# Thirty-two 128x128 turns a layer leave TensorE: VectorE turns 32x32 blocks and a trip through DRAM puts them in place

## The chip, the cores and the metric

The kernel runs on one core of a Trainium2 chip. That core has five engines, each with its own instruction queue: TensorE (PE in the profile; its weight loads are PEld), VectorE (DVE), ScalarE (ACT), GpSimd (POOL) and SyncE (SP), which here only issues DMAs. Sixteen DMA engines move data between DRAM and the on-chip memory; a DMA is issued by SP, ACT or POOL and waits in that engine's queue until its semaphores are met. Matmul results land in PSUM, from which ACT or DVE must copy them.

The metric is the device time of one execution, in microseconds, as a median over several executions. Before the change it is 1737.33 us, from 1736.18 to 1737.69 us.

## The reference

The kernel computes two layers of a decoder trunk over a sequence of 512 positions and 1024 channels. In each layer a normalized input goes through one wide projection, whose columns feed three branches and three sets of gates; the gated sum of the branches is projected and added, and a gated MLP with a short convolution follows. Two of the branches matter here.

```
# recurrence (8 heads of 64):  S_t = S_{t-1} (diag(w_t) - kk_t^T (a_t kk_t)) + v_t^T k_t ;  y_t = S_t r_t
y = rwkv7_scan(r, decay, k, v, kk, a)
mean, var = over the 64 channels of a head
y = (y - mean) * rsqrt(var + 64e-5) * lnx_g + lnx_b
y = y + sum(r * k * r_k) * v
return y * g

# retention (4 heads, q and k of 64 channels, chunks of 128 positions)
q, k = rotary(q), rotary(k) / 8
scores = (q_i . k_j) * decay_in[i, j]     # within a chunk
inner  = scores @ v
kv     = k^T (v * k_dec)                  # carried from chunk to chunk
cross  = q @ R_prev * q_dec
y = (inner + cross) normalized, times silu(g)
```

In both there is a turn from positions on the partitions to channels on the partitions. The recurrence's `y` is normalized with positions on the partitions, since a head's channels then lie along a row; the branch projection wants channels on the partitions. The rotation of q and k works with positions on the partitions, since the tables of cosines are per position; the products `q . k` contract over channels and want those on the partitions.

## The kernel before

Activations are kept as features: 128 channels on the partitions, 512 positions along a row. Weights come from DRAM in pieces of 128x512 (256 KB) through three raw buffers (`wr`), are cut by ACT (`wh` or `sh`, line 134) and DVE (`wl` or `sl`, line 135) into a high and a low part in a reduced-precision format, and each product of a weight piece and an activation is three matmuls (line 151, `mm3`). Almost the whole time goes into these. Weight pieces are prepared ahead of their use by a fixed number of pieces, two during the recurrence, three or more later.

The order on each engine is set when the program is built: the scheduler of the framework places instructions by a simulated time, except where the code pins them (`keep_in_program_order`, in the code often `po`). The engines then run their queues strictly in that order, waiting on semaphores.

In each layer the work around the change runs so:

- **Recurrence** (`rwkv`). Eight steps, c = 0 to 7, of 64 positions. A step's chain goes PE, DVE (`XB`), PE, ACT (`U`), PE, DVE (the state `S`, lines 628 and 629), and the next step's first products read `S` (line 563). Between the parts of a chain stand fillers, each one weight piece of 12 matmuls of the gates' and retention's projections (`fill`, lines 151). After every odd step the 128 finished positions `y` are normalized: DVE takes sums (lines 639 to 646), POOL raises to the power -1/2 (`rs`, line 648), DVE multiplies (line 649). The four tiles `y` stay in memory.
- **Rotation** (`rotate`, lines 780 to 785). While the recurrence runs, four tiles of 128 positions of q and k are rotated on DVE into `ro`, using a second tile `rb_`.
- **Read-out** (`rwkv_out`). After the recurrence, PE runs four groups of 24 products for the spatial gating branch (`sgu_v`), and between them, for each of four blocks of 128 channels, four transposes of `y` into one PSUM tile (line 661), a copy out by ACT with scale and bias (line 663), and DVE's additions and products (lines 664 and 667).
- **Retention's heads** (`ret_heads`). Some ten microseconds later PE turns the four `ro` tiles in sixteen transposes (line 796) into `qF` and `kF`, which ACT and DVE copy out (line 798). The rows of the retention (`ret_row`, line 817) read them.

So a layer has 32 transposes of 128x128 on PE. In layer 2 everything is repeated with the same order.

The last layer's MLP already has a turn by DVE's 32x32 blocks and a trip through DRAM (`turn_x`, lines 963 to 968): DVE transposes blocks of 32x32 (`xz`), SP writes them to DRAM in pieces of 512 bytes (`xr<-xz`, line 966) and reads them back in pieces of 128 bytes (`xt<-xr`, line 968).

Of the kernel before, what the change touches and what calls it, by code (L numbers as in the profile page):

```python
# [8 lines left out]
F32 = mybir.dt.float32  # L9
F32R = mybir.dt.float32r  # L10
AF = mybir.ActivationFunctionType
# [7 lines left out]
NC = 4  # L19
# [28 lines left out]
class Emit:  # L48
# [343 lines left out]
        return self.fp.tile(list(shape), dt, name=self.nm(n), tag="a")  # L392


    def rwkv(self, l, nst):
        nc, V, A, a = self.nc, self.nc.vector, self.nc.scalar, self.a
        T, P = nc.tensor, nc.gpsimd
# [3 lines left out]
        po = self.tc.keep_in_program_order if l == 0 else lambda i: i  # L401
# [33 lines left out]
        for i in range(2):  # L435
            x = self.u(n="wax")
            for h in range(2):
                o, s = x[64 * h:64 * h + 64, :], wa[64 * i:64 * i + 64, :]
# [12 lines left out]
        hv, po = [slice(0, 64), slice(64, 128)], self.tc.keep_in_program_order  # L451
# [105 lines left out]

        Vt, yT, mh = [None] * 8, [], [(m, h) for m in range(4) for h in range(2)]  # L560

        def mm(o, l, r, start=False):
            po(T.matmul(o, l, r, start=start, stop=True, skip_group_check=True))  # L563
# [17 lines left out]
        for c in range(8):  # L581
            if c % 2 == 0:
                y = self.r(n="y")
# [22 lines left out]
            for i in (0, 4, 5, 6, 7, 1, 2, 3):  # L606
                for h in range(2):
                    m, o = i % 4, 1 - h
# [14 lines left out]
            if c < 7:  # L623
                f = F[:, :, c:c + 1].to_broadcast([128, 4, 64])
# [17 lines left out]
            sq = self.r(n="ysq")  # L642
# [4 lines left out]
            rs = self.small((128, 8), "rs8")  # L647
            nc.gpsimd.tensor_tensor(rs, s2, self.c("mhalf")[:, 0:8], op=POW)
            V.tensor_tensor(h8(y), h8(y), rs.unsqueeze(2).to_broadcast([128, 8, 64]), op=MUL)
            yT.append(y)  # L650
        return yT, bv, gd

    def rwkv_out(self, l, yT, bv, gd):
        nc, V, A, T, a = self.nc, self.nc.vector, self.nc.scalar, self.nc.tensor, self.a
        gw, gx = self.split(self.gup, self.f), self.split(gd, self.f)
        self.yrw = []
        for m in range(4):
            ms = slice(m * 128, m * 128 + 128)
            pt = self.sm()
            for c in range(NC):  # L660
                self.tc.keep_in_program_order(T.transpose(pt[:, c * 128:c * 128 + 128], yT[c][:, ms], self.c("ident")))  # L661
            t = self.f(n="yF")
            A.activation(t, pt, AF.Identity, scale=self.p("lg", m), bias=self.p("lb", m))
            V.tensor_tensor(t, t, bv[m], op=ADD)
            pg = self.sm()
            self.mm3(pg, (gw[0][:, ms], gw[1][:, ms]), gx, True, True)
            V.tensor_tensor(t, t, pg, op=MUL)
            self.yrw.append(self.split(t, self.f))
            yield
# [96 lines left out]
    def rotate(self, l, qs):  # L766

        nc, V, a, po = self.nc, self.nc.vector, self.a, self.tc.keep_in_program_order
        for c in range(NC):
            s = qs.pop(0)  # L770
            if c % 2 == 0:
                tab = [self.u((128, 2, 256), n="tab") for _ in range(2)]
                for i in range(2):
                    nc.scalar.dma_start(tab[i], a["rot"][:, i, c:c + 2, :])
            src = s.rearrange("p (h e d) -> p h e d", e=2, d=32)
            Cc, Ss = [t[:, c % 2, :].rearrange("p (h d) -> p h d", d=32) for t in tab]
            o = self.u(n="ro")
            ov = o.rearrange("p (h e d) -> p h e d", e=2, d=32)
            b = self.u((128, 8, 2, 32), n="rb_")
            po(V.tensor_tensor(ov, src, Cc.unsqueeze(2).to_broadcast([128, 8, 2, 32]), op=MUL))  # L780
            po(V.tensor_tensor(b[:, :, 0, :], src[:, :, 1, :], Ss, op=MUL))
            yield
            po(V.tensor_tensor(b[:, :, 1, :], src[:, :, 0, :], Ss, op=MUL))
            po(V.tensor_tensor(ov[:, :, 0, :], ov[:, :, 0, :], b[:, :, 0, :], op=SUB))
            po(V.tensor_tensor(ov[:, :, 1, :], ov[:, :, 1, :], b[:, :, 1, :], op=ADD))
            self.ro.append(o)
            yield

    def ret_heads(self):

        A, V, T, po = self.nc.scalar, self.nc.vector, self.nc.tensor, self.tc.keep_in_program_order
        self.qF, self.kF = [], []
        for j in range(4):
            pt = self.sm((128, 4, 128))
            for c in range(NC):
                po(T.transpose(pt[:, c, :], self.ro[c][:, j * 128:j * 128 + 128], self.c("ident")))
            t = self.r((128, 4, 128), n="qF" if j < 2 else "kF")
            (V.tensor_copy if j % 2 else A.copy)(t, pt)
            (self.qF if j < 2 else self.kF).append(t)
        self.kd = []  # L800
        for c in range(NC - 1):
            kd = self.r((128, 4, 64), n="kd")
            V.tensor_tensor(kd, self.ro[c][:, 256:512].rearrange("p (h d) -> p h d", d=64),
                            self.c("kdec").unsqueeze(2).to_broadcast([128, 4, 64]), op=MUL)
            self.kd.append(kd)
# [396 lines left out]
```

## Time and profile before

| | us |
|---|---|
| median of three executions | 1737.33 |
| the profiled execution, its own time | 1736.33 |
| its span, first to last instruction | 1734.6 |
| PE busy | 1725.1 |
| DVE busy | 1121.2 |
| ACT busy | 775.8 |
| POOL busy | 151.9 |
| recurrence with its normalizations, layer 1 | about 214 to 317 |
| read-out and heads, layer 1 | about 344 to 381 |
| the same in layer 2 | about 1074 to 1177 and 1204 to 1241 |

A row of a timeline gives the start in us from the beginning of the span, the duration, the engine, the line, the operation, the tile written and the tiles read, and in brackets the idle time of the engine before it and what ended that. A row of a line or a tile gives the least, the median and the greatest duration in ns. Matmuls are pipelined: the distance between two starts, not the duration, is what one costs PE.

### The profile page before, as it was taken

What the parts mean: (1) busy time and instruction counts of PE and PEld (TensorE: products, weight loads), DVE (VectorE), ACT (ScalarE), POOL (GpSimd) and SP (SyncE); (2) the same over time, 40 slices, a digit from 0 to 9 for tenths busy, and PEclk for the clock granted to TensorE, in tenths of its full rate; (3) what the DMA queues carried; (4) which work ended last, traced back from release to release, by engine and by line L of the source; (5) the groups of instructions that cost most, each with busy time, mean ns of one, the idle gap of its engine ahead of it and who ended that gap; (6) DMA issues with size and microseconds to landing.
All of it is one profiled execution on the core that took longest, in us unless ns stands there. A gap on an engine that the chain in (4) does not pass through costs nothing.

```text
span 1734.6 us, 27538 instructions
## 1 busy us (share of the span) xinstructions
PE 1725.1 (99%) x10544; PEld 1421.0 (82%) x10544; DVE 1121.2 (65%) x1933; ACT 775.8 (45%) x1329; POOL 151.9 (9%) x168
## 2 busy tenths in 40 slices
PE   9999999999999999999999999999999999999998
PEld 7888877888888888888888888778888888888887
DVE  6777645568658777753357785455686698876432
ACT  6554444534345444443255635445343454443322
POOL 1011000002300000000021210000132000000010
PEclk9999999999999999999999999999999999999999
DMA  5234433424543223233332344234154444432431
GB/s 178 86 98 140 134 98 94 134 66 163 162 145 98 97 97 96 69 116 112 116 116 73 98 146 124 92 115 129 59 176 143 152 128 122 121 110 73 152 99 54
DMA packets 124900, 198.64 MB, mean 115 GB/s; under 512 B 29408, under 2 KB 35296, under 8 KB 124768
## 3 DMA queue, kind: packets, MB, share of 16 engines
q1 hardware_dynamic: 110064, 164.15, 30.1%
q10 hardware_dynamic: 10224, 18.05, 3.1%
q0 software_dynamic: 4480, 14.68, 2.6%
q8 instruction: 83, 1.36, 0.3%
q14 instruction: 49, 0.40, 0.1%
HBM read 177.95 MB, written 18.87 MB: 113 GB/s over the span
## 4 chain that ended last, share of the span: by engine, by line
PE 97%; DMA 1%; DVE 1%; ACT 0%; issue 0%; ACTq 0%; DVEq 0%
PE acc L151 86%; PE sm L151 4%; PE sm L563 2%; PE sm L817 1%; PE sm L507 1%; DMA wr<-wall 0%; PE sm L922 0%; PE sm L590 0%; DMA x<-xT 0%; PE sm L479 0%; PE sm L468 0%; PE sm L467 0%; PE sm L845 0%; PE sm L661 0%; PE sm L872 0%
## 5 line engine op out<-in xcount | busy, mean ns | idle before, releaser
L151 PE MATMUL acc<-lo,sh 128*128 128x512 f32 x1108 | 432.6, 391 | 0.0
L151 PE MATMUL acc<-hi,sh 128*128 128x512 f32 x1108 | 431.6, 390 | 0.0
L151 PE MATMUL acc<-hi,sl 128*128 128x512 f32 x1108 | 430.5, 389 | 0.0
L134 ACT CAST sh<-wr 128x512 fp32r<-128x512 f32 (+1 forms) x385 | 235.4, 616 | 390.4 <-PE acc L151 286.8
L135 DVE TENSOR_TENSOR sl<-wr,sh 128x512 fp32r<-128x512 f32 (+1 forms) x385 | 263.4, 688 | 177.9 <-ACT sh L134 108.0
L151 PEld LDWEIGHTS acc<-lo,sh 128*128 128x128 f32 x1108 | 208.0, 188 | 43.9 <-issue 0.7
L151 PEld LDWEIGHTS acc<-hi,sl 128*128 128x128 f32 x1108 | 208.0, 188 | 43.3
L151 PEld LDWEIGHTS acc<-hi,sh 128*128 128x128 f32 x1108 | 208.1, 188 | 42.7 <-issue 0.2
L151 PE MATMUL acc<-lo,wh 128*128 128x512 f32 x588 | 232.9, 396 | 0.8 <-DVE lo L210 0.6
L151 PE MATMUL acc<-hi,wl 128*128 128x512 f32 x588 | 229.7, 391 | 0.0
L151 PE MATMUL acc<-hi,wh 128*128 128x512 f32 x588 | 229.6, 390 | 0.0
L135 DVE TENSOR_TENSOR wl<-wr,wh 128x512 fp32r<-128x512 f32 x195 | 141.8, 728 | 133.8 <-ACT wh L134 132.9
L134 ACT CAST wh<-wr 128x512 fp32r<-128x512 f32 x195 | 120.7, 619 | 218.4 <-PE acc L151 208.0
L151 PEld LDWEIGHTS acc<-lo,wh 128*128 128x128 f32 x588 | 110.5, 188 | 25.8 <-DVE lo L210 1.2
L151 PEld LDWEIGHTS acc<-hi,wl 128*128 128x128 f32 x588 | 110.4, 188 | 23.9 <-issue 0.7
L151 PEld LDWEIGHTS acc<-hi,wh 128*128 128x128 f32 x588 | 110.6, 188 | 22.2 <-issue 0.3
L151 PE MATMUL acc<-ah,sh 128*128 128x512 f32 x352 | 108.4, 389 | 0.0
L989 DVE TENSOR_TENSOR fu<-acc,rsF 128x512 f32<-128x512 f32 x88 | 60.8, 690 | 66.1 <-PE acc L151 66.0
L991 ACT ACTIVATE cv<-fu,pc 128x512 f32<-128x512 f32 x88 | 71.7, 816 | 47.6 <-DVE fu L989 45.1
L992 DVE SCALAR_TENSOR_TENSOR cv<-fu,pc,cv 128x511 f32<-128x511 f32 x88 | 65.7, 748 | 19.9 <-ACT cv L991 19.8
L151 PE MATMUL acc<-wl,hi 128*128 128x512 f32 x192 | 78.3, 408 | 0.0
L151 PEld LDWEIGHTS acc<-ah,sh 128*128 128x128 f32 x352 | 66.1, 188 | 13.6
(297 smaller groups left out, 2338.5 us busy)
## 6 DMA issues: line engine op xcount, KB each, us to landing
wr<-wall SPq DMA_DIRECT2D x488, 256.0 KB, 2.6
gd<-gth ACTq DMA_DIRECT2D x48, 256.0 KB, 2.9
gth<-gd POOLq DMA_DIRECT2D x48, 256.0 KB, 3.5
wr<-wdt SPq DMA_DIRECT2D x44, 256.0 KB, 2.8
wr<-wdn SPq DMA_DIRECT2D x40, 256.0 KB, 2.7
tab<-rot ACTq DMA_DIRECT2D x8, 256.0 KB, 3.5
xi<-xT SPq DMA_DIRECT2D x8, 256.0 KB, 3.3
xd<-xi POOLq DMA_DIRECT2D x8, 256.0 KB, 2.7
```

What stands on the lines that cost most here:

```text
L134: self.kept(self.nc.scalar.copy(hi[:, :n], raw[:, :n]))
L135: self.kept(self.nc.vector.tensor_tensor(lo[:, :n], raw[:, :n], hi[:, :n], op=SUB))
L151: i = self.nc.tensor.matmul(*x, **y, **kw)
L507: i = T.matmul(pK[hv[1 - h], j, :], bk[hv[h], c, 1, :], x[hv[h], c, :], start=True, stop=True)
L563: po(T.matmul(o, l, r, start=start, stop=True, skip_group_check=True))
L817: po(T.matmul(X[h][:, i, :], lhsT, rhs, start=new[h], stop=stop, skip_group_check=True))
L989: V.tensor_tensor(u, ps, self.rsF, op=MUL)
L991: A.activation(t, u, AF.Identity, scale=self.p("cw2", j), bias=self.p("cb", j))
L992: V.scalar_tensor_tensor(t[:, 1:], u[:, :511], self.p("cw1", j), t[:, 1:], op0=MUL, op1=ADD)
```

## The change

The four finished tiles `y` of the recurrence and the four rotated tiles `ro` are no longer kept for PE. As soon as one is finished, `to_dram` lets DVE transpose its sixteen 32x32 blocks per 32 positions in one instruction over 128x512, into a tile that is no longer needed (`ysq` or `rb_`), and POOL issues four DMAs, each of 32 partitions with 16 x 32 runs of 32 numbers (512 pieces of 128 bytes, 64 KB), that write the blocks to their places in a 512x512 array in DRAM (`tn`). Later, SP reads four tiles of 128 channels x 512 positions back from it for `yF`, and four for `qF` and `kF`, each a DMA of 256 KB. The transposes on PE and the copies out of PSUM by lines 663 (which becomes an in-place scaling of `yF`) and 798 go. Nothing else is computed differently.

```
+    def to_dram(self, z, src, d, c, eng):
+        self.nc.vector.transpose(z.rearrange("p (b t) -> p b t", t=32), src.rearrange("p (b f) -> p b f", f=32))
+        for q in range(4):
+            eng.dma_start(d.rearrange("(b f) t -> f b t", f=32)[:, :, 128 * c + 32 * q:128 * c + 32 * q + 32],
+                          z[32 * q:32 * q + 32].rearrange("f (b t) -> f b t", t=32))
+    def turned(self):
+        return self.dp.tile([512, 512], F32, name=self.nm("tn"))
...
-        Vt, yT, mh = [None] * 8, [], [(m, h) for m in range(4) for h in range(2)]
+        Vt, yT, mh = [None] * 8, self.turned(), [(m, h) for m in range(4) for h in range(2)]
...
             V.tensor_tensor(h8(y), h8(y), rs.unsqueeze(2).to_broadcast([128, 8, 64]), op=MUL)
-            yT.append(y)
+            self.to_dram(sq, y, yT, c // 2, nc.gpsimd)
...
-        self.yrw = []
-        for m in range(4):
+        self.yrw, ys = [], [self.f(n="yF") for _ in range(4)]
+        for m, t in enumerate(ys):
+            nc.sync.dma_start(t, yT[128 * m:128 * m + 128, :])
+        for m, t in enumerate(ys):
             ms = slice(m * 128, m * 128 + 128)
-            pt = self.sm()
-            for c in range(NC):
-                self.tc.keep_in_program_order(T.transpose(pt[:, c * 128:c * 128 + 128], yT[c][:, ms], self.c("ident")))
-            t = self.f(n="yF")
-            A.activation(t, pt, AF.Identity, scale=self.p("lg", m), bias=self.p("lb", m))
+            A.activation(t, t, AF.Identity, scale=self.p("lg", m), bias=self.p("lb", m))
...
+        self.qk = self.turned()
...
+            self.to_dram(b.rearrange("p h e d -> p (h e d)"), o, self.qk, c, nc.gpsimd)
             self.ro.append(o)
...
-            pt = self.sm((128, 4, 128))
-            for c in range(NC):
-                po(T.transpose(pt[:, c, :], self.ro[c][:, j * 128:j * 128 + 128], self.c("ident")))
             t = self.r((128, 4, 128), n="qF" if j < 2 else "kF")
-            (V.tensor_copy if j % 2 else A.copy)(t, pt)
+            self.nc.sync.dma_start(t.rearrange("p c t -> p (c t)"), self.qk[128 * j:128 * j + 128, :])
```

The lines of the changed file are 10 later in the recurrence, 8 or 9 later in the read-out and the rotation, 7 later from the heads on: line 648 is 658, line 649 is 659, 628 is 638.

The scheduler places the new instructions among the old ones. At three places of layer 1 (layer 2 has the same order) the queues read as follows; the first number of a row is the line, a tile's numbers are its buffers.

POOL during the recurrence, before: the four powers `rs`, one for each pair of steps, and then the first of the spatial gating branch's.

```order
L648 TENSOR_TENSOR rs_491_2543<-s_490_2540,con 128x8
L648 TENSOR_TENSOR rs_533_2851<-s_532_2848,con 128x8
L648 TENSOR_TENSOR rs_569_3151<-s_568_3148,con 128x8
L648 TENSOR_TENSOR rs_611_3431<-s_610_3428,con 128x8
L890 TENSOR_TENSOR brs_3835<-bve_3833,con 128x1
```

POOL at the same place with the change (`x4` is four DMAs).

```order
L399 DMA tn_2211<-ysq_2852 32x16x32 x4
L399 DMA tn_3193<-rb__583_3199 32x16x32 x2
L658 TENSOR_TENSOR rs_570_3162<-s_569_3159,con 128x8
L399 DMA tn_3193<-rb__583_3199 32x16x32 x2
L399 DMA tn_2211<-ysq_3157 32x16x32 x4
L399 DMA tn_3193<-rb__595_3308 32x16x32 x4
L399 DMA tn_3193<-rb__606_3398 32x16x32 x4
L658 TENSOR_TENSOR rs_613_3463<-s_612_3460,con 128x8
L399 DMA tn_3193<-rb__618_3491 32x16x32 x4
L399 DMA tn_2211<-ysq_3458 32x16x32 x4
```

Two DMAs of the first rotated tile now stand ahead of the third `rs`, and fourteen more between the third and the fourth.

DVE from the third normalization's sum to the state's update of step c = 6, before.

```order
L645 TENSOR_REDUCE s_568_3148<-ysq_3146 128x8
L646 TENSOR_SCALAR s_568_3148<-s_568_3148 128x8
L135 TENSOR_TENSOR wl_3270<-wr_3159,wh_3269 128x512
L780 TENSOR_TENSOR ro_3285<-qs_3115,tab_3177 128x512
L781 TENSOR_TENSOR rb__593_3286<-qs_3115,tab_3178 128x8x32
L649 TENSOR_TENSOR y_2854<-y_2854,rs_569_3151 128x512
L135 TENSOR_TENSOR wl_3312<-wr_3212,wh_3311 128x512
L783 TENSOR_TENSOR rb__593_3286<-qs_3115,tab_3178 128x8x32
L784 TENSOR_TENSOR ro_3285<-ro_3285,rb__593_3286 128x8x32
L628 TENSOR_TENSOR S_396<-S_396,sm_3233 128x256
```

The same stretch with the change.

```order
L655 TENSOR_REDUCE s_569_3159<-ysq_3157 128x8
L397 STREAM_TRANSPOSE rb__583_3199<-ro_3198 128x512
L656 TENSOR_SCALAR s_569_3159<-s_569_3159 128x8
L135 TENSOR_TENSOR wl_3292<-wr_3175,wh_3291 128x512
L789 TENSOR_TENSOR ro_3307<-qs_3126,tab_3194 128x512
L790 TENSOR_TENSOR rb__595_3308<-qs_3126,tab_3195 128x8x32
L659 TENSOR_TENSOR y_2865<-y_2865,rs_570_3162 128x512
L397 STREAM_TRANSPOSE ysq_3157<-y_2865 128x512
L135 TENSOR_TENSOR wl_3334<-wr_3229,wh_3333 128x512
L792 TENSOR_TENSOR rb__595_3308<-qs_3126,tab_3195 128x8x32
L793 TENSOR_TENSOR ro_3307<-ro_3307,rb__595_3308 128x8x32
L638 TENSOR_TENSOR S_396<-S_396,sm_3255 128x256
```

One transpose now stands ahead of the scaling of the sum that POOL waits for, and one between the product with `rs` and the state.

SP in the read-out with the change; before, only the weight loads `wr` stand there.

```order
L668 DMA yF_3924<-tn_2211 128x512
L121 DMA wr_3832<-wall 128x512
L668 DMA yF_3925<-tn_2211 128x512
L121 DMA wr_3838<-wall 128x512
L668 DMA yF_3926<-tn_2211 128x512
L121 DMA wr_4058<-wall 128x512
L668 DMA yF_3927<-tn_2211 128x512
L805 DMA qF_4077<-tn_3193 128x512
L805 DMA qF_4079<-tn_3193 128x512
L805 DMA kF_4081<-tn_3193 128x512
L121 DMA wr_4094<-wall 128x512
L805 DMA kF_4083<-tn_3193 128x512
```

The first `yF` waits for all sixteen writes of its array, and the last `kF` stands behind a weight load.

## The prediction

> **What bounds the kernel now.** I read the page's busy times first, then its chain of waits, then PE's timeline at the places that change.
>
> ```profile
> PE 1725.1 (99%) x10544; PEld 1421.0 (82%) x10544; DVE 1121.2 (65%) x1933; ACT 775.8 (45%) x1329; POOL 151.9 (9%) x168
> PE 97%; DMA 1%; DVE 1%; ACT 0%; issue 0%; ACTq 0%; DVEq 0%
> ```
>
> PE is busy 1725.1 of 1734.6 us and makes 97% of the chain that ended last. Every microsecond taken out of PE's queue is gained, and every microsecond for which PE is made to wait is lost; the other engines have room, but not at every moment. The next view is the same by stretches, for the end of the recurrence and for the read-out of layer 1.
>
> ```profile
> 284.00:320.00 36.00, 36.00 (x344) 28.51 (x343) 22.86 (x48) 14.34 (x27) 4.32 (x2) 1.00 0.35 111
> 340.00:385.00 45.00, 45.00 (x228) 37.69 (x227) 27.89 (x55) 17.47 (x29) 4.02 (x7) 1.00 0.24 78
> ```
>
> The columns are the stretch, its length, then busy time (and instructions) of PE, PEld, DVE, ACT and POOL, the granted clock, the DMA engines' share and GB/s. PE is busy without a gap in both, at full clock; POOL does 4 us of work in each, the DMA engines are a third and a quarter busy.
>
> **What the change removes.** PE's timeline around one group of four transposes, and around the sixteen of the heads:
>
> ```profile
> 353.08 0.39 PE L151 MATMUL acc<-sh,lo 128*128 128x512 f32 x1
> 353.31 0.60 PE L661 MATMUL sm<-con,y 128*128 128x128 f32 x4
> 353.67 0.48 PE L151 MATMUL sm<-lo,hi 128*128 128x512 f32 x1
> 353.98 0.40 PE L151 MATMUL sm<-hi,hi 128*128 128x512 f32 x1
> 378.54 0.39 PE L151 MATMUL acc<-hi,sl 128*128 128x512 f32 x1
> 378.77 0.38 PE L796 MATMUL sm<-con,ro 128*128 128x128 f32 x2
> 380.43 0.48 PE L151 MATMUL acc<-lo,sh 128*128 128x512 f32 x1
> 380.75 0.39 PE L151 MATMUL acc<-hi,sh 128*128 128x512 f32 x1
> ```
>
> An ordinary matmul takes 0.23 us from start to start (353.08 to 353.31). From the first transpose of four to the second matmul behind them it is 353.98 - 353.31 = 0.67, so the four cost 0.67 - 0.23 = 0.44. The sixteen cost 380.75 - 378.77 - 0.23 = 1.75 (the row of 378.77 shows two of them). Eight groups of four and two of sixteen in both layers: 8 x 0.44 + 2 x 1.75 = **7.0 us** less in PE's queue. The copies out of PSUM on ACT and DVE that go with the heads, and the scaling of `yF`, which only reads another memory, ran beside a busy PE; I count nothing for them.
>
> **What it adds, and where that waits.** Per layer, eight transposes of 128x512 on DVE, 32 DMAs on POOL and eight on SP. For the transposes the nearest rows are the existing ones, a quarter and twice the size:
>
> ```profile
> L963 DVE STREAM_TRANSPOSE xz<-xi x32: 267/274/315, 1389.9 to 1536.2; 128x128 f32<-128x128 f32 x32
> L708 DVE STREAM_TRANSPOSE cs<-cs x2: 2218/2221/2224, 187.5 to 1047.7; 128x1024 f32<-128x1024 f32 x2
> ```
>
> Four times 0.274 is 1.10, half of 2.22 is 1.11; I take 1.1 us. For POOL's issue of 512 pieces of 128 bytes there is no row. POOL's present issues carry 256 KB in rows of 2 KB; SP issues both kinds of shape:
>
> ```profile
> L934 POOL DMA_DIRECT2D gth<-gd x48 | 26.6, 557 | 0.1
> L968 SPq DMA_DIRECT2D xt<-xr x32: 360/448/529, 1393.2 to 1541.0; - x32
> 346.00 0.33 SPq L121 DMA_DIRECT2D wr<-wall  x1
> DMA to landing us min/median/max: 2.0/2.6/3.9
> DMA to landing us min/median/max: 2.8/3.5/6.4
> ```
>
> (The fourth row belongs to `xt<-xr`, the fifth to `gth<-gd`.) Bounds for POOL: 0.56 us if the pieces cost nothing, 4 x 0.56 = 2.2 us if an issue grows with its pieces, 512 instead of 128. On SP the same step from 128 to 512 pieces takes 0.33 to 0.45, a factor of 1.36. I take 0.56 x 1.36 = **0.75 us**, since SP's row is the only one with this shape of transfer.
>
> That matters at one place in each layer: step c = 6 of the recurrence. DVE's and PE's timeline there, in layer 1, and POOL's `rs`:
>
> ```profile
> 288.10 0.68 DVE L645 TENSOR_REDUCE s<-ysq 128x8 f32<-128x512 f32 x1
> 288.82 0.17 DVE L646 TENSOR_SCALAR s<-s 128x8 f32<-128x8 f32 x1
> 289.14 2.05 POOL L648 TENSOR_TENSOR rs<-s,con 128x8 f32<-128x8 f32 x1 [24.60 <-DVE s L646]
> 291.22 0.69 DVE L649 TENSOR_TENSOR y<-y,rs 128x512 f32<-128x512 f32 x1 [0.58 <-POOL rs L648]
> 293.04 0.69 DVE L135 TENSOR_TENSOR wl<-wr,wh 128x512 fp32r<-128x512 f32 x1 [1.13 <-ACT wh L134]
> 294.32 0.42 DVE L628 TENSOR_TENSOR S<-S,sm 128x256 f32<-128x256 f32 x1
> 294.99 0.42 DVE L629 TENSOR_TENSOR S<-S,F 128x256 f32<-128x256 f32 x1
> 295.86 0.34 PE L563 MATMUL sm<-S,X 64*64 64x64 f32 x8
> ```
>
> `S` is ready at 295.41 and PE reads it at 295.86, without a gap before: a margin of 0.45 us. With the change the transpose of the rotated tile comes in at 288.8 and ends at 289.9; then POOL's two writes of it stand ahead of `rs`: 289.9 + 2 x 0.75 + 2.05 = 293.45, against 291.2 now. DVE waits for it in front of `y`, and behind that wait stand the second transpose, a weight split, the rotation and `S`. From `y` at 293.5, 0.6 until the next start and 1.1 for the transpose bring the split to 295.2 instead of 293.04: DVE's two idle stretches (0.58 and 1.13) are eaten up and `S` comes 2.15 us late. PE waits 2.15 - 0.45 = 1.7 us. Layer 2 has the same order but more room:
>
> ```profile
> 1148.39 1.63 POOL L648 TENSOR_TENSOR rs<-s,con 128x8 f32<-128x8 f32 x1 [24.06 <-DVE s L646]
> 1152.85 0.69 DVE L135 TENSOR_TENSOR wl<-wr,wh 128x512 fp32r<-128x512 f32 x1 [1.81 <-ACT wh L134]
> 1154.79 0.42 DVE L629 TENSOR_TENSOR S<-S,F 128x256 f32<-128x256 f32 x1
> 1155.66 0.34 PE L563 MATMUL sm<-S,X 64*64 64x64 f32 x8
> ```
>
> There `rs` starts at 1148.39, 0.3 behind the sum; a transpose from 1148.1 on ends at 1149.2, POOL's two writes at 1150.7, `rs` at 1152.3, `y` and the transpose behind it at 1154.0; the split starts then instead of 1152.85, `S` is 1.15 late, and PE waits 0.7. Together **2.4 us** of waiting; with an issue of 0.56 it is 1.6, with 2.2 it is 2.4 + 4 x 1.45 = 8.2.
>
> The other added steps I cost at nothing, with this cover. The transposes at the other odd steps fall into idle time of DVE, or into the two weight pieces by which it is ahead: the split of 293.04 above is first used by the matmuls at 300.58. The last `rs` of the layer has fourteen writes ahead of it since the third; these take 14 x 0.75 = 10.5 us from about 293.5, and it is due at 314.14. The last writes are issued by about 326 and land 3.5 to 6.4 us later, by 332; SP comes to the first `yF` after the weight load of 346.00, so it has 14 us to spare. Without that cover SP would stand still with weight loads behind it, and these are not wanted soon: the next one that ACT casts is cast at 368.42.
>
> ```profile
> 300.58 4.99 PE acc L151 x21
> 314.14 2.28 POOL L648 TENSOR_TENSOR rs<-s,con 128x8 f32<-128x8 f32 x1 [22.95 <-DVE s L646]
> 368.42 0.61 ACT L134 CAST sh<-wr 128x512 fp32r<-128x512 f32 x1
> 369.94 0.33 SPq L121 DMA_DIRECT2D wr<-wall  x1
> 383.78 0.38 PE L817 MATMUL sm<-qF,kF 64*128 64x128 f32 x2
> ```
>
> The last `kF` stands behind the weight load of 369.94, lands some 3 us later and is wanted at 383.78. ACT's scaling of the first two `yF` now stands ahead of the first copy of the gating branch and makes that one or two microseconds late; nobody waits for it within ten.
>
> **The sum.** 1736.33 (the profiled execution's own time) - 7.0 + 2.4 = 1731.7. The median of the runs is 1.0 above that execution, so I predict **1732.7 us**, 4.6 less or 0.27%.
>
> **Rivals.** *All hidden*: POOL's two writes and the transposes cost PE nothing, because `rs` or DVE's queue runs closer than the rows say. For it: the margins and idle stretches are there. Against it: they add up to 0.45 + 0.58 + 1.13 us in layer 1, less than two transposes and two issues. Then the change is worth its 7.0: 1730.3.
>
> *POOL's issues are held up by DVE*: its writes fall into a stretch in which DVE works without a break, and if each waits for one DVE instruction of 0.69 us the issue costs 1.44 and the wait at `S` grows by 4 x 0.69 = 2.8, to 5.2: 1735.5, no change that can be told. The only row with POOL issues beside DVE work, `gth` at 371.28, shows three in 1.85 us while DVE ran 0.55 us of a scaling and then additions:
>
> ```profile
> 371.28 1.85 POOL L934 DMA_DIRECT2D gth<-gd  x3
> 371.30 0.55 DVE L891 TENSOR_SCALAR sgv<-sgv,bmv,brs 128x512 f32<-128x512 f32 x1 [0.72 <-POOL brs L890]
> ```
>
> Three ordinary issues take 1.67, so it was held by 0.2 us at most. The Trainium skill (SBUF — State Buffer, section "SBUF: two separate sides") describes such a lock: VectorE in one of its two-port modes keeps GpSimd from writing descriptors. By that page these DMAs would better be issued from SP; by its rule the time would be this rival's. The trace agrees that an issue can be lengthened, but by little.
>
> *POOL's issue grows with the pieces*, 2.2 us each: the wait at `S` takes 8.2 us in both layers. Then the fourteen writes between the third and the fourth `rs` take 31 us; in layer 1 the third ends at 296.4, so the fourth cannot end before 329.9, where it would be due at about 321 (316.4 now, and 4.6 by which everything is late). DVE stands nine microseconds in front of `y`, with the weight splits behind it; these are 7 us ahead of PE (293.04 to 300.58), so PE waits some 2 us more per layer. 1737.3 - 7.0 + 8.2 + 4 = 1742.5, slower. It decides the sign from 1.9 us an issue on, where 2.4 + 4 x 1.15 equals 7.0. Against it stands SP's factor of 1.36, for it that POOL's queue is of another kind than SP's:
>
> ```profile
> q1 hardware_dynamic: 110064, 164.15, 30.1%
> q0 software_dynamic: 4480, 14.68, 2.6%
> ```
>
> **How the numbers follow.** A difference of under 0.2% (3.5 us) can't be told from none in this kernel. The forecast has a chance of 0.44 (0.36 of it below 1733.9, the rest within 0.2%), all hidden 0.18, held up by DVE 0.20, growing with the pieces 0.18. So faster 0.54, same 0.28, slower 0.18. The range goes from half a microsecond under the all-hidden case, 1729.8, to 1742; what is left out is half of the slow case and a little below. The forecast's own range is 1730.5 to 1734.5.
>
> **What would show it.** PE without lines 661 and 796 and 64 matmuls fewer. POOL's rows of line 399 at 0.6 to 0.9 us. A gap of PE before the products with `S` at about 294 to 298 in layer 1 and 1150 to 1158 in layer 2, 1 to 2 us long and nowhere else; `rs` behind two DMAs. SP's `yF` issued right behind the weight load, with no wait for POOL's writes. I am wrong if POOL's issues take over 1.4 us, if PE waits at the merges behind the read-out (then `yF` or `kF` is late), or if PE's gaps lie at the weight splits.

## The result, and the profile after

The changed kernel takes **1731.94 us** (median of 16 runs, 1730.61 to 1737.14), the kernel before, run beside it, 1737.02 us (1735.62 to 1738.54). The ratio is 0.9973, with a 95% interval of 0.9966 to 0.9980: faster by 0.27%. Measured a second time (e5 below) it is 0.9976, 0.9967 to 0.9985. The prediction was 1732.7 us.

The profiled execution took 1731.78 us, its span is 1730.1 against 1734.6 before. The page's busy times, and the shares of the chain that ended last, of the changed kernel:

```profile
PE 1717.9 (99%) x10480; PEld 1414.5 (82%) x10480; DVE 1125.9 (65%) x1945; ACT 774.2 (45%) x1325; POOL 193.8 (11%) x232
PE 96%; DMA 1%; DVE 1%; POOL 1%; issue 0%; ACT 0%; SPq 0%; ACTq 0%; POOLq 0%; DVEq 0%
```

PE still sets the end. It makes 64 matmuls fewer and is busy 7.2 us less (1725.1 - 1717.9), but the span is only 4.5 us shorter. POOL appears in the chain where it was not before. The same two stretches as in the prediction:

```profile
284.00:320.00 36.00, 33.91 (x331) 26.56 (x329) 24.50 (x52) 14.21 (x27) 15.61 (x21) 1.00 0.51 130
340.00:385.00 45.00, 45.00 (x215) 37.22 (x214) 30.52 (x61) 20.22 (x32) 4.42 (x7) 1.00 0.44 140
```

At the end of the recurrence PE is busy 33.91 of 36 us: it has holes of 2.1 us that the kernel before did not have. At the read-out it has none. The DMA engines' share went from 0.35 to 0.51 and from 0.24 to 0.44. What PE waited for over the whole execution, in the kernel before and then in the changed one:

```profile
PE acc L274 <- DVE rst L271: 1.5, 1, 1.5
PE acc L151 <- DVE lo L210: 0.6, 2, 0.3
```

```profile
PE acc L274 <- DVE rst L271: 1.5, 1, 1.5
PE acc L151 <- DVE wl L135: 1.4, 2, 1.1
PE sm L573 <- DVE S L639: 1.1, 2, 0.9
PE acc L151 <- DVE lo L210: 0.9, 3, 0.5
```

The columns are microseconds in all, times, and the longest. The first and the last row lie in the first 10 us of the program, and the kernel before has them too. The other two are new: products with the state `S` (the wait that was forecast), and products with the low part `wl` of a weight (a wait that was not). PE's timeline in layer 1, at the first place in the kernel before, and then at both in the changed one:

```profile
295.54 0.39 PE L151 MATMUL acc<-wh,lo 128*128 128x512 f32 x1
295.86 0.34 PE L563 MATMUL sm<-S,X 64*64 64x64 f32 x8
```

```profile
295.53 0.39 PE L151 MATMUL acc<-wh,lo 128*128 128x512 f32 x1
296.86 0.35 PE L573 MATMUL sm<-S,X 64*64 64x64 f32 x9 [0.94 <-DVE S L639]
318.57 0.39 PE L151 MATMUL acc<-wh,lo 128*128 128x512 f32 x1
320.03 0.51 PE L151 MATMUL acc<-wl,hi 128*128 128x512 f32 x1 [1.07 <-DVE wl L135]
```

Before, the first step takes 0.32 us from start to start and the second 0.23 (317.58 to 317.81, in the rows of before further down). Here they take 1.33 and 1.46: PE loses 1.0 us at `S` and 1.2 at the split. In layer 2 the same two steps take 0.59 and 0.73, a loss of 0.27 and 0.50. That makes 3.0 us of waiting in all. All losses below are worked out like this, from the same two steps of PE.

**The first wait.** POOL and VectorE at step 6 of layer 1, and the two new instructions' own times:

```profile
290.03 1.29 POOL L399 DMA_DIRECT2D tn<-rb__583_3199  x2 [21.24 <-DVE s L656]
291.33 1.66 POOL L658 TENSOR_TENSOR rs<-s,con 128x8 f32<-128x8 f32 x1
293.03 0.69 DVE L659 TENSOR_TENSOR y<-y,rs 128x512 f32<-128x512 f32 x1 [1.71 <-POOL rs L658]
293.75 0.71 DVE L397 STREAM_TRANSPOSE ysq<-y 128x512 f32<-128x512 f32 x1
294.39 0.65 DVE L135 TENSOR_TENSOR wl<-wr,wh 128x512 fp32r<-128x512 f32 x1
296.29 0.42 DVE L639 TENSOR_TENSOR S<-S,F 128x256 f32<-128x256 f32 x1
L399 POOL DMA_DIRECT2D tn<-ysq x32: 648/648/876, 242.3 to 1179.7; - x32
L397 DVE STREAM_TRANSPOSE ysq<-y x8: 703/711/712, 240.9 to 1176.5; 128x512 f32<-128x512 f32 x8
```

It is the forecast chain: two writes of 0.65 us stand ahead of `rs`, VectorE waits 1.71 us for it in front of `y`, then turns the read-out tile, splits a weight, goes on with the rotation, and only then comes to `S`. `S` starts at 296.29, 1.30 us later than the 294.99 of before.

**The second wait.** VectorE in layer 1 behind the recurrence, first in the kernel before, with the matmul that uses the split (the last row) and the one ahead of it:

```profile
311.35 0.69 DVE L335 TENSOR_TENSOR ws<-ws,con 128x512 f32<-128x512 f32 x1 [2.08 <-DMA ws<-sgw]
316.45 0.69 DVE L649 TENSOR_TENSOR y<-y,rs 128x512 f32<-128x512 f32 x1 [1.52 <-POOL rs L648]
317.06 1.28 DVE L135 TENSOR_TENSOR wl<-wr,wh 128x512 fp32r<-128x512 f32 x2
317.58 0.39 PE L151 MATMUL acc<-wh,lo 128*128 128x512 f32 x1
317.81 0.49 PE L151 MATMUL acc<-wl,hi 128*128 128x512 f32 x1
```

and the same in the changed kernel:

```profile
313.56 0.69 DVE L335 TENSOR_TENSOR ws<-ws,con 128x512 f32<-128x512 f32 x1 [3.30 <-DMA ws<-sgw]
316.35 2.30 POOL L658 TENSOR_TENSOR rs<-s,con 128x8 f32<-128x8 f32 x1 [9.87 <-DVE s L656]
318.68 0.69 DVE L659 TENSOR_TENSOR y<-y,rs 128x512 f32<-128x512 f32 x1 [0.81 <-POOL rs L658]
319.29 0.68 DVE L135 TENSOR_TENSOR wl<-wr,wh 128x512 fp32r<-128x512 f32 x1
```

In both kernels VectorE's queue stops at the mask of `ws`, the matrix `sgw`, until its load lands. Behind the mask stand the sum for the fourth `rs`, then `y`, then the weight split. All of them moved by the same 2.2 us (311.35 to 313.56, 316.45 to 318.68, 317.06 to 319.29). The fourth `rs` itself was not held by POOL's writes: POOL had been idle for 9.87 us. From the split's start to the matmul it is 0.75 us before, without a wait, and 0.74 now, with one: **before the change this split came exactly in time in layer 1**, without a margin, and nothing in the profile shows that as a wait. The mask is late because the load is. The three loads at the recurrence's end, issue to landing in us, of the kernel before and then of the change:

```profile
gup<-gup SPq DMA_DIRECT2D x1, 256.0 KB, 2.8
bs<-sgb SPq DMA_DIRECT2D x1, 256.0 KB, 4.0
ws<-sgw SPq DMA_DIRECT2D x1, 256.0 KB, 4.2
```

```profile
gup<-gup SPq DMA_DIRECT2D x1, 256.0 KB, 5.0
bs<-sgb SPq DMA_DIRECT2D x1, 256.0 KB, 5.2
ws<-sgw SPq DMA_DIRECT2D x1, 256.0 KB, 5.4
```

Of the 2.2 us, 1.0 come from the first wait (the load is issued at 308.12 instead of 307.12), and PE itself is late by as much, so they cost nothing more. The other 1.2 come from the landing, and they are the loss at the split.

### The profile page after: what moved, and what is told of

It reads as the page before. It is cut to its first block, busy times and chain, and to the rows that moved or that the text cites. A ratio compares the mean times of both kernels' runs of the same rounds, so it can differ in the third digit from the quotient of the medians.

```text
span 1730.1 us, 27554 instructions
## 1 busy us (share of the span) xinstructions
PE 1717.9 (99%) x10480; PEld 1414.5 (82%) x10480; DVE 1125.9 (65%) x1945; ACT 774.2 (45%) x1325; POOL 193.8 (11%) x232
## 4 chain that ended last, share of the span: by engine, by line
PE 96%; DMA 1%; DVE 1%; POOL 1%; issue 0%; ACT 0%; SPq 0%; ACTq 0%; POOLq 0%; DVEq 0%
PE acc L151 85%; PE sm L151 4%; PE sm L573 2%; PE sm L824 1%; PE sm L517 1%; DMA ws<-sgw 1%; POOL rs L658 0%; DMA tab<-rot 0%; PE sm L929 0%; PE sm L489 0%; PE sm L600 0%; DVE wl L135 0%; DMA x<-xT 0%; PE sm L478 0%; PE sm L477 0%
```

## The experiments

Theory T was: the transposes are worth some 7 us of PE; 3 us of that come back as two separate waits, at `S` because two writes stand ahead of the third `rs` on POOL, and at the split because `sgw` lands late. The rivals: the additions cost nothing and the removal is worth less (A); VectorE's transposes, not POOL's writes, make `S` late (B); the second wait has nothing to do with the load (C); the two waits are one (E); the landing times vary by themselves (F).

### e1: the removal alone

```diff
-            pt = self.sm()
-            for c in range(NC):
-                self.tc.keep_in_program_order(T.transpose(pt[:, c * 128:c * 128 + 128], yT[c][:, ms], self.c("ident")))
+            pt = yT[m]
...
-            pt = self.sm((128, 4, 128))
-            for c in range(NC):
-                po(T.transpose(pt[:, c, :], self.ro[c][:, j * 128:j * 128 + 128], self.c("ident")))
+            pt = self.ro[j].rearrange("p (c t) -> p c t", c=4)
```

> The kernel before without its 64 transposes on TensorE; the read-out, q and k are taken from the unturned tiles, so the output is not the reference's; no transposes on VectorE and no trip through DRAM. Theory T (the removal is worth the 7.0 us of the prediction and the additions cost the waits of PE, 3.0 us in the profile of the changed kernel): 7.0 us faster than before, 1730.0, and no wait of PE at the products with S of step 6 nor at the weight split behind the fourth rs. Rival A (the removal alone is worth only the 4.5 to 5 us that were measured, since PE then waits elsewhere, and the additions cost nothing): 1732.3.

Measured: 1728.77 us against 1736.54 of the kernel before, 7.8 us faster; ratio 0.9955, 0.9941 to 0.9968. PE's two steps are 0.32 and 0.23 us again in both layers. Rival A's 1732.3 (a ratio of 0.9976) lies outside the interval. So the whole removal is gained where nothing is put in its place, and what is added costs 3 us or so. The traces give the removal more closely than the times: matched one by one with those of the kernel before, PE's matmuls gain 3.6 us in the read-out and the heads of each layer (345 to 400 us, 1205 to 1260), in e1 and in the change alike, which makes 7.2 us.

### e2 and e9: one half of the change each

e2 keeps the part of `rwkv` and `rwkv_out` and takes q and k back to TensorE:

```diff
-        self.qk = self.turned()
...
-            self.to_dram(b.rearrange("p h e d -> p (h e d)"), o, self.qk, c, nc.gpsimd)
...
+            pt = self.sm((128, 4, 128))
+            for c in range(NC):
+                po(T.transpose(pt[:, c, :], self.ro[c][:, j * 128:j * 128 + 128], self.c("ident")))
-            self.nc.sync.dma_start(t.rearrange("p c t -> p (c t)"), self.qk[128 * j:128 * j + 128, :])
+            (V.tensor_copy if j % 2 else A.copy)(t, pt)
```

e9 does the reverse: `yT.append(y)` and the transposes of `rwkv_out` as before, q and k as in the change.

> Only the recurrence's read-out goes by VectorE's transposes and through DRAM; q and k are turned by TensorE as before. Theory T: half the transposes (8 groups of four, 3.5 us) are gone, no write of a rotated tile stands ahead of the third rs, none is in flight when sgw is loaded: S of step 6 in time, sgw lands 4.2 us after its issue as before, no wait of PE, 3.5 us faster than before, 1733.5. Rival B (the transposes on VectorE themselves, 0.70 us ahead of S, make PE wait): the wait before the products with S is there, 0.7 us or more over both layers, and 1734.2 or more.

> Only q and k go by VectorE's transposes and through DRAM; the read-out is turned by TensorE as before. Theory T: 3.5 us of transposes gone (two times 1.75); two writes still stand ahead of the third rs, but no turn of a read-out tile (0.65 us) between it and S: wait before the products with S 1.0 - 0.65 = 0.4 us in layer 1 and none in layer 2; the third rotated tile's writes are under way with the three loads, the first of them lands 3.4 to 5.0 us after its issue, wait at the split 0.5 to 1.2 us in layer 1 and 0.2 to 0.5 in layer 2. Gain 3.5 - 1.7 = 1.8 us, 1734.7; with the 3.3 of e2 that makes the 4.5 to 5.1 of the whole change. Rival A (the additions cost nothing): 3.5 us, 1733.0.

Measured: e2 1733.25 us, 3.3 faster (ratio 0.9983, 0.9974 to 0.9991); e9 1734.36 against 1736.93 of the kernel before beside it, 2.6 faster (0.9983, 0.9974 to 0.9992). The times alone cannot tell e9's 1.8 us from its rival's 3.5; PE's steps can. e9 loses 0.39 us at `S` in layer 1 and none in layer 2, and 0.55 and 0.81 at the split. All four are about what was written down, the last a little more.

e2 loses nothing at `S`, but 0.57 and 0.51 us at the split, which theory T had at nothing. There `sgw` lands 4.0 us after its issue, as before. VectorE of e2 shows the cause:

```profile
315.75 0.69 DVE L659 TENSOR_TENSOR y<-y,rs 128x512 f32<-128x512 f32 x1 [1.56 <-POOL rs L658]
316.48 0.71 DVE L397 STREAM_TRANSPOSE ysq<-y 128x512 f32<-128x512 f32 x1
317.11 1.86 DVE L135 TENSOR_TENSOR wl<-wr,wh 128x512 fp32r<-128x512 f32 x3
```

In this kernel's order the turn stands ahead of the split: from `y` to the split it is 1.36 us (315.75 to 317.11), where the kernel before has 0.61 (316.45 to 317.06), and the split has next to no margin. Rival B is right in its mechanism, at another place than it named: a transpose on VectorE costs PE its own time where it stands ahead of a split that comes just in time. In the changed kernel that turn stands behind the split.

### e3: the third rs ahead of the first rotated tile's writes

```diff
-            eng.dma_start(d.rearrange(...
+            self.tc.keep_in_program_order(eng.dma_start(d.rearrange(...
...
-            nc.gpsimd.tensor_tensor(rs, s2, self.c("mhalf")[:, 0:8], op=POW)
+            po(nc.gpsimd.tensor_tensor(rs, s2, self.c("mhalf")[:, 0:8], op=POW))
```

> The changed kernel with POOL's order fixed: the third rs ahead of the first rotated tile's writes, instead of two of them ahead of it. The order of every other engine is the same. Theory T: the third rs starts 1.3 us (two issues) earlier, S of step 6 is in time in both layers, the waits of 1.0 and 0.27 us before its products go; the second wait, at the weight split behind the fourth rs, stays at about 1.2 and 0.5 us, since the rows that feed it only move 1.0 us forward with PE. 1.3 us faster than the change, 1730.6. Rival B (VectorE's transposes ahead of S make it late): S late as now, 1731.9.

Measured: 1730.78 us (ratio 0.9965, 0.9952 to 0.9977). POOL and VectorE of e3 at step 6 of layer 1:

```profile
289.45 1.97 POOL L658 TENSOR_TENSOR rs<-s,con 128x8 f32<-128x8 f32 x1 [20.41 <-DVE s L656]
291.45 0.69 DVE L659 TENSOR_TENSOR y<-y,rs 128x512 f32<-128x512 f32 x1 [0.62 <-POOL rs L658]
292.18 0.71 DVE L397 STREAM_TRANSPOSE ysq<-y 128x512 f32<-128x512 f32 x1
294.79 0.42 DVE L639 TENSOR_TENSOR S<-S,F 128x256 f32<-128x256 f32 x1
```

The turn is still between `y` and `S`, and `S` starts at 294.79, earlier than in the kernel before. PE's step at `S` is 0.32 us in both layers: the wait is gone, and with it rival B at this place. The split still loses 1.0 us in layer 1. In layer 2 it loses nothing, and there `sgw` landed 4.2 us after its issue; in layer 1 it took 5.2.

### e4 and e8: sgw first

```diff
         with self.tc.high_priority():
+            self.nc.sync.dma_start(self.ws, self.a["sgw"][l])
             self.nc.sync.dma_start(self.gup, self.a["gup"][l])
         self.nc.sync.dma_start(self.bs.rearrange("p g i -> p (g i)"), ...
-        self.nc.sync.dma_start(self.ws, self.a["sgw"][l])
```

e4 is this edit on the changed kernel, e8 on the kernel before.

> The changed kernel with the load of sgw as the first of the three loads at the recurrence's end instead of the third; VectorE and ScalarE take its mask and split one or two places earlier in their orders. Theory T (the second wait of PE comes from the late landing of sgw, behind which the fourth rs and the weight split stand): sgw lands about 1 us earlier, the split of the weights no longer stands behind the fourth rs, the waits of 1.2 and 0.5 us go, the waits before S stay: 1.7 us faster than the change, 1730.2. Rival C (the second wait comes from POOL's writes or VectorE's transposes beside it, not from the load): unchanged, 1731.9.

> The kernel before with the load of sgw first, as in e4. Theory T (the late landing costs PE only where the change made it late): no wait of PE there before or now, same time, 1736.5. Rival G (the order of the loads is worth the 2 us of e4 in any kernel): 1734.5.

Measured: e4 1729.97 us (ratio 0.9961, 0.9948 to 0.9973). `sgw` lands 3.4 us after its issue, both losses at the split are gone, those at `S` are there (1.01 and 0.69 us). Rival C, by which nothing should have changed, falls. The edit does two things, though: the load is first, and the splits no longer stand behind the fourth `rs`; e4 does not tell their shares. That the landing accounts for the loss shows in the landings of all runs, below the table at the end of this section. e8 takes 1736.86 us, ratio 1.0002, 0.9993 to 1.0011: without the change the same edit is worth nothing, since nothing is late there (rival G falls). Its profiled execution, 1738.12 us, has the 1.8 us by which it is behind that of the kernel before at other places: at the program's start, at 288 us and at 935 us.

### e5 and e6: the change again, and both edits together

> The changed kernel itself, on the chip of the next three runs, so that they can be compared with it directly. All theories: 4.5 to 5.1 us faster than the kernel before, as it was; its waits at the products with S and at the weight split are there again in both layers, 2.5 to 3.5 us in sum.

> The changed kernel with the third rs ahead of the first rotated tile's writes and the load of sgw first: the edits of e3 and e4 together. Theory T (two separate waits, each with its own cause): the gains add up, 1.2 + 2.0 = 3.2 us faster than the change, 1728.7, and no wait of PE over 0.2 us at either place. Rival E (one wait feeds the other, so that either edit takes most of both): not faster than e4, 1730.

Measured on one chip: the change 1732.09 us (ratio 0.9976, 0.9967 to 0.9985), both edits **1728.80 us** (0.9954, 0.9941 to 0.9966). The intervals do not meet. The change again loses 1.02 and 0.47 us at `S`, but only 0.43 and 0.21 at the split; the three loads took 3.9, 4.4 and 4.6 us in layer 1 this time, not 5.0, 5.2 and 5.4. The loss at the split thus varies with the landing from one execution to the next; the profiled one, at 1730.58 us, is the shortest of these runs, so it shows less waiting than the median has. With both edits PE waits at neither place:

```profile
PE acc L274 <- DVE rst L271: 1.5, 1, 1.5
PE acc L151 <- DVE lo L210: 0.5, 2, 0.3
```

These are all of its rows in that view. The gains add up (1.2 + 2.0 forecast, 3.3 measured): two waits with a cause each, not one (rival E). This version beats both kernels and comes to what e1 gained without any turn at all.

### e7: no writes under way when the loads are issued

On top of e3, the third rotated tile's four writes come with the fourth's:

```diff
-            self.to_dram(b.rearrange("p h e d -> p (h e d)"), o, self.qk, c, nc.gpsimd)
+            zs.append(b.rearrange("p h e d -> p (h e d)")); self.to_dram(zs[c], o, self.qk, c, nc.gpsimd, [(zs[i], i) for i in ((0,), (1,), (), (2, 3))[c]])
```

> The edit of e3, and the third rotated tile's four writes issued only behind the fourth rs, so that none of them is under way when the three loads at the recurrence's end are issued; VectorE then turns the last read-out tile one place earlier, ahead of the weight split. Theory T (the loads land late because the writes of 128-byte pieces are on the DMA engines with them): the first load lands 2.5 to 3.0 us after its issue and sgw 4.0 to 4.2, as in the kernel before, in place of 4.3 to 5.0 and 4.7 to 5.4; the wait at the split falls to the 0.6 and 0.4 us of e2, where the turned tile stands ahead of the split too; 2 us faster than the change, 1729.9. Rival F (the landing times vary by themselves or with where the loads are issued): sgw 4.7 us or more, the wait at the split 1 us or more in layer 1, 1731.

Measured: 1729.62 us (ratio 0.9961, 0.9947 to 0.9975). The loads of e7 in layer 1:

```profile
gup<-gup SPq DMA_DIRECT2D x1, 256.0 KB, 2.7
bs<-sgb SPq DMA_DIRECT2D x1, 256.0 KB, 3.5
ws<-sgw SPq DMA_DIRECT2D x1, 256.0 KB, 4.0
```

In layer 2 they take 3.0, 3.3 and 3.9. Over all kernels with `gup` first, that first load lands 2.5 to 3.0 us after its issue where no rotated tile was written shortly before (before, e1, e2, e7: eight loads) and 3.1 to 5.0 where one was (the change twice, e3, e9, e10: ten). With `sgw` first it is 2.6 and 3.0 in e8, without such writes, and 3.3 to 3.4 in e4 and e6. Rival F falls. The Trainium skill (DMA: Bandwidth & Descriptors, section "Issuing engines are not separate DMA queues") says that DMAs of all issuing engines run on the same 16 DMA engines and interleave; these landings agree with it. At the split e7 loses 0.51 and 0.46 us, as forecast from e2: the turn stands ahead of it here too.

### e10: the rotated tiles' writes issued by SP

```diff
-            self.to_dram(b.rearrange("p h e d -> p (h e d)"), o, self.qk, c, nc.gpsimd)
+            self.to_dram(b.rearrange("p h e d -> p (h e d)"), o, self.qk, c, nc.sync)
```

> The changed kernel with the rotated tiles' writes issued by SP's queue, which loads the weights, in place of POOL's; VectorE turns the last read-out tile one place earlier, ahead of the weight split, as in e7. Theory T: the third rs is free of them, the wait before S goes in both layers (1.3 us); the writes are still under way with the three loads, so these land late as in the change (first load 3.4 us or more) and with the turn ahead of the split the wait there is 1.0 to 1.8 us in layer 1 and 0.5 to 1.0 in layer 2: 1731 to 1732. Rival H (a write in SP's queue that waits for VectorE holds the weight loads behind it): a wait of PE for weights that is in no other run, some us, 1734 or more. Rival I (what delays the loads is POOL's way of issuing, not the pieces): first load at 2.5 to 3.0 us, 1730.

Measured: 1730.34 us (ratio 0.9964, 0.9950 to 0.9979). No loss at `S`; 1.19 and 0.43 us at the split. The first load lands after 3.5 us in layer 1 and 3.1 in layer 2, `sgw` after 4.6 and 3.9. Rival H, a wait for weights, does not show. Rival I is not borne out in layer 1, where the last write landed 0.7 us after the first load's issue and the load is as late as with POOL's writes in e9. Layer 2 is no test of it, since the writes were not under way there as was assumed: the last one landed at 1162.71, and the first load was issued at 1162.86. Another queue thus takes away the first wait, which was a matter of POOL's order. Of the second, the turn ahead of the split, which costs e2 and e7 0.46 to 0.57 us with the load in time, is all of layer 2's 0.43 and more than half of layer 1's 1.19; only the rest of 0.4 comes from the late landing.

### All runs at a glance

Losses of PE against the kernel before's steps, and landings, in layer 1 / layer 2, from the profiled execution of each. The medians come from four sets of runs, in which the kernel before took 1736.5 to 1737.0 us; its row gives the one beside the change.

| kernel | median us | loss at `S` | loss at the split | first load | `sgw` |
|---|---|---|---|---|---|
| before | 1737.0 | 0 / 0 | 0 / 0 | 2.8 / 2.5 | 4.2 / 4.0 |
| change | 1731.9 | 1.01 / 0.27 | 1.23 / 0.50 | 5.0 / 4.3 | 5.4 / 4.7 |
| change again (e5) | 1732.1 | 1.02 / 0.47 | 0.43 / 0.21 | 3.9 / 4.0 | 4.6 / 4.4 |
| e1 removal alone | 1728.8 | 0 / 0 | 0 / 0 | 2.6 / 2.6 | 4.0 / 4.1 |
| e2 only `y` | 1733.3 | 0 / 0 | 0.57 / 0.51 | 3.0 / 3.0 | 4.0 / 4.0 |
| e3 `rs` first | 1730.8 | 0 / 0 | 1.00 / 0 | 4.7 / 3.7 | 5.2 / 4.2 |
| e4 `sgw` first | 1730.0 | 1.01 / 0.69 | 0 / 0 | (sgw) | 3.4 / 3.4 |
| e6 both | 1728.8 | 0 / 0 | 0 / 0 | (sgw) | 3.3 / 3.3 |
| e7 writes held | 1729.6 | 0 / 0 | 0.51 / 0.46 | 2.7 / 3.0 | 4.0 / 3.9 |
| e8 before, `sgw` first | 1736.9 | 0 / 0 | 0 / 0 | (sgw) | 2.6 / 3.0 |
| e9 only q, k | 1734.4 | 0.39 / 0 | 0.55 / 0.81 | 3.6 / 4.5 | 4.7 / 5.0 |
| e10 SP issues | 1730.3 | 0 / 0 | 1.19 / 0.43 | 3.5 / 3.1 | 4.6 / 3.9 |

The last column accounts for the loss at the split in every run whose split stands behind the mask and the fourth `rs`. In layer 1 of the kernel before `sgw` lands 4.21 us after its issue and the split is just in time. Where the split follows `y` at once, as there (the change, e3, e5 and e9), the loss is the landing less 4.21 us, to within 0.03 us in all eight cases: a landing of 5.42 leaves 1.21, and 1.23 are lost; one of 4.16 leaves nothing, and nothing is lost. Where the turn stands between (e2, e7 and e10), 0.75 us more go from `y` to the split, and the loss is the landing less 4.21 plus 0.75, again to within 0.03 in all six. Nothing is left for POOL's queue or for VectorE's other turns at this place. By the same sum the split had 0.2 us to spare in layer 2 of the kernel before, where `sgw` landed after 4.03.

## Why the prediction was right, and where not

**PE bounds, and what leaves its queue is gained (7.0 us).** Right. PE's busy time fell by 7.2 us, PE's matmuls gain 7.2 us at the places of the transposes, and e1 gained 7.8 (5.6 to 10.2 by its interval). The Trainium skill (VectorE: DVE Perf Modes, section "Rules for kernel authors") advises TensorE for a 128x128 turn whose result may go to PSUM; in this kernel TensorE is the one engine without room, and e6 shows the turn cheaper elsewhere.

**The price of a transpose (1.1 us).** Too high: 0.70 to 0.71. Four times the small row and half of the strided one agreed with each other and were both wrong. Interpolating between two shapes does not give a third.

**The price of an issue on POOL (0.75 us).** Near: 0.65 by the median, 0.88 at most in 64. It does not grow with the pieces as that rival (0.18) had it, which falls, and no issue of the changed kernel took the 1.44 us that the other one (0.20) reckoned with one VectorE instruction of 0.69 in front, so that one falls too.

**The wait at `S` (2.4 us over both layers).** Right in place, cause and layer order, shown by e3; the size was 1.3 (1.5 in e5). In layer 1 `S` came 1.30 us late, not 2.15. Row by row: the writes start at 290.03, where 289.9 was reckoned, for the transpose is 0.4 us shorter, but the sum ahead of it stands 0.3 later (288.44 instead of 288.10, behind the late tables spoken of below); the two issues take 1.29 instead of 1.5; `rs`, carried over with 2.05, takes 1.66; and from `y` to the split it is 1.36 instead of 1.7, since the second transpose is shorter. The margin was sized too large as well: PE reads `S` 0.15 us after its end even where it waits for it (296.71 and 296.86), so 0.30 of the 0.45 us were to spare, and 1.30 less 0.30 is the 1.0 that PE lost. So the rival that all is hidden (0.18), whose 1730.3 is nearer to the result than its reasons deserve, was wrong: PE does wait.

**"The other added steps I cost at nothing."** This is the step that failed. It cost 1.7 us, and 0.6 in e5, at the weight split behind the fourth `rs`; the text had named that as a sign of its being wrong. It looked for cover at this place on POOL, rightly, since POOL was idle there; it did not ask what the writes do to other transfers, nor whether the split behind `rs` has a margin. e7 shows the first, the rows of before show the second: none in layer 1, 0.2 us in layer 2.

**The sum.** Overpricing the one wait by 1.1 us and leaving out the other, 1.7 us, nearly cancel; 7.2 less 3.0 makes 4.2, where the span shows 4.5 and the medians 5.1. That the time was within 0.8 us of the forecast is luck to that extent: one wait was sized too large by about as much as the other was overlooked.

**What stays open.** By PE's matmuls, matched one by one, some 0.2 us at the start of the program, 0.2 at 207 us and 0.35 at 935 us of the gain lie far from the change; e1 to e7 have the last two in nearly the same size, and the first between nothing and 0.6. e8, which is the kernel before but for one load, has nothing of the 0.2 at 207 us, and it is 0.8 us later than the kernel before at the start and 0.7 at 935 us: so the start and 935 us vary by as much without the change, and what gains the 0.2 is not known. A third, smaller loss of 0.4 us in layer 1, in the change, e4, e5 and e6, comes at the copy `XB` of step 6 (287.77 instead of 287.44): the rotation's tables landed some 4.3 us after their issue there and 3.4 to 3.8 in before, e1, e2, e3 and e7. e8 loses 0.6 us there, with tables that landed after 4.5, so this loss comes without the change too; why the tables are late was not tried. Nor is it shown how the writes hold the first load. In layer 1 of the change the load was issued at 307.26, the last write landed at 309.02, and the load only at 312.22, 3.2 us later; that is longer than a whole load takes where no such writes are near (2.5 to 3.0). And no run writes the same bytes in larger pieces, so whether the small pieces or the bytes hold it is open.

## What to carry to other kernels

Work taken from the engine that bounds is gained in full; what decides is the handful of places where something hands work to that engine just in time, so read the margin of each of them near the change, also of those that the change does not touch: a margin of nothing does not show as a wait. A transfer that is off every path can still delay the loads issued behind it, and where one such load stands at the head of an in-order queue its lateness reaches everything in that queue. When small DMA issues are put on an engine with a latency-critical instruction, fix their order by hand: two edits of a line or two were worth 3.3 us here, the whole change 4.4 on the same chip.

## What the hardware showed that was not expected

A 32x32-block transpose of 128x512 on VectorE takes 0.70 us, while 128x128 takes 0.27 and a strided 128x1024 takes 2.22: the time is not proportional to the elements across these forms.

The writes in small pieces took the DMA engines longer for their bytes than the loads do. In 276 to 330 us POOL's queue holds the 24 writes of the changed kernel and nothing else: 1.57 MB, whose packets took 15.1% of the time of all sixteen engines (the first row below). That is 8.2 of 54 us, about 190 GB/s. The queue of the loads moved 164.15 MB in 30.1% of 1734.6 us in the kernel before, about 314 GB/s. The two differ in direction as well as in their pieces, and no run tells these apart.

How the pieces appear depends on the queue. POOL's queue in the changed kernel, 276 to 330 us (packets, MB, share), and then the packets of e10 from 280 on:

```profile
q0 software_dynamic: 768, 1.57, 15.1%
```

```profile
DMA packets 11787, 7.28 MB, mean 146 GB/s; under 512 B 8912, under 2 KB 8912, under 8 KB 11780
```

From POOL a write of 64 KB in 512 pieces is 32 packets of 2 KB (768 for 24 writes); from SP the pieces are packets of their own (sixteen writes are most of the 8912 packets under 512 bytes). SP's issue of one took 0.41 to 0.60 us by the median of a tile, POOL's 0.65.
